# Hybrid attention and linear-attention step on one core: a ring of small weight slots, 512-wide products, and first sums over half of the mix

## The chip, the core and the metric

The kernel runs on one core of a Trainium2 chip. A core has five engines that work side by side, each through its own instructions in order: TensorE (PE, matrix products; PEld is its loading of the stationary operand), VectorE (DVE), ScalarE (ACT), GpSimd (POOL) and SyncE (SP), which issues most of the DMAs. They wait for each other through semaphores. The metric is the device time of one execution in microseconds (us). One further execution was recorded by the hardware profiler; times within the program are from that one.

## What is computed

Two layers over 2048 prompt tokens and 8 x 16 sample tokens, model width 1024. Each layer projects the normalised input into nine parts, runs sliding-window attention and gated linear attention side by side, multiplies both by gates, projects the joined result (the "mix") back, and adds a gated input embedding:

```python
xn = rms_norm(h, norm_g)
u = xn @ w_in
qa, ka, va, ga, qb, kb, vb, gb, ab = jnp.split(u, _split_points(), axis=-1)
...                                   # q and k: norm per head, partial rotary
oa = swa_prompt(qa, ka, va, sinks)    # or swa_sample with the cache
...
logg = jax.nn.log_sigmoid((ab @ w_gate_up + b_gate).astype(jnp.float32)) / GATE_TAU
ob, s_new = gla_recurrent(qb, kb, vb, logg, s0)
ob = rms_norm(ob, gla_norm_g)
mix = jnp.concatenate([oa.reshape(bn, L, A_WIDTH) * jax.nn.silu(ga),
                       ob.reshape(bn, L, B_WIDTH) * jax.nn.silu(gb)], axis=-1)
h = h + mix @ w_out
gate = jax.nn.sigmoid(rms_norm(h, pe_norm_g) @ w_pg)
h = h + gate * (p_l @ w_pe)
```

The widths of the parts are 512, 128, 128, 512, 256, 256, 512, 512 and 16 columns.

## The kernel before

**Tiling.** The 17 tiles of 128 tokens (the last one holds the samples) are worked off in five groups of 3, 4, 4, 3 and 3 tiles, for each of two layers; so there are ten groups and 34 passes of a tile. A group runs `phase_in` (projections, attention, linear attention) and then `phase_out` (output projection, gate).

**Products.** Every weight and every activation is split into a high and a low part, and every product runs as three matmuls per slice of 128 rows (k): high by high, high by low, low by high. These are the three source lines L343, L344 and L345 in `mm3`. With eight k a unit has 24 matmuls. `unit_b` holds 128 tokens stationary and streams weight columns (kv 272 wide; q0, q1, vb0, vb1, gb0, gb1 256 wide). `unit_a` holds 128 weight columns stationary and streams the group's 384 or 512 tokens (ga, qb, kb, and in `phase_out` o0 to o3 over the mix, g0 to g3 over the activations `A` and `B`, and e0 to e3 with two k over the embedding `phl`).

**Weights.** They come by DMA in pieces of two k by 256 columns (256 KB) into four `raw` buffers. `w_split` makes the high part on ScalarE (L175) and the low part on VectorE (L95). There are two whole-block buffers `w`, and two of the small ones `we`. `w_ahead` issues splits of the next block while the present one runs. From the end of the o blocks on, splits are held behind the last square of the mean (`wgate`).

**Order.** Attention and linear attention are generators that are advanced a step at a time (`pump`) between projection units. A list scheduler then sets each engine's instruction order from the program's order and its own estimates. Attention is finished (`drain`) after vb, linear attention after gb. A linear attention tile ends so: products into the PSUM pair `o` and state products into `t`; squares of `o` on ScalarE (L798, four); a scale and a power on GpSimd (L799, L801); four products into `on` on VectorE (L804); four transposes on TensorE (L815); then ScalarE (L817) and VectorE (L818) write them into the second half of the mix, `mix1`. The first half, `mix0`, is the attention's. PSUM has two banks for `mm`, two for `t`, and four that are used either as two pairs, `s` and `o`, or as four single banks `pw`.

Of the kernel before, what the change touches and what calls it, by code (L numbers as in the profile page):

```python
# [8 lines left out]
F32 = mybir.dt.float32  # L9
# [14 lines left out]
Z = dict(eg=0, gk=2, yp=1, ym=6, pga=1, pqk=1, pvb=2, pgb=3, pG=3, pgb0=0, lanes=2, keepk=1, keepq=-1, tga=2, wo=-1,  # L24
         y1=1, y2=1, y3=1, ya=1, yb=1, raw=4, hx=4, vbe=2, po0=6, wah=0, th=3)
# [21 lines left out]
def hybrid_step(ctx: ExitStack, tc: tile.TileContext, a: dict, o: dict):  # L47
# [54 lines left out]
    def pw(n=512):  # L102

        rot[0] += 1
        if rot[0] % 3 == 1:
            return pm(n)
        return banks["pool"].tile([128, 512], F32, tag="w", name="pw", bufs=4)[:, :n]
# [5 lines left out]
    def chain(prev, after=(), **kw):  # L113

        if prev[0] is None:
            prev[0] = PE.matmul(**kw).ins  # L116
# [10 lines left out]

    plan = []
    for l in range(DEPTH):
        for gi in range(len(GROUPS)):  # L130
            for nm, wd in IN_BLOCKS:
                off = IN_OFF[nm][0]
                plan.append((l, gi, nm, 8, wd, a["w_in"][l, :, off:off + 8 * wd].rearrange("p (k c) -> p k c", k=8)))
            for b in range(4):
                plan.append((l, gi, f"o{b}", 8, 256, a["w_out"][l, :, b]))
            for b in range(4):
                plan.append((l, gi, f"g{b}", 8, 256, a["w_pg"][l, :, b]))
                plan.append((l, gi, f"e{b}", 2, 256, a["w_pe"][l, :, b]))
    pieces = []
    for bi, (_, _, nm, K, wd, src) in enumerate(plan):  # L140
        for k0 in range(0, K, 2):
            pieces.append((bi, k0, src[:, k0:k0 + 2, :], wd))
# [5 lines left out]
    wtiles = {}  # L148
    raws = {}
    st = dict(dma=0, split=0, blk=0)  # L150
    wgate = [None]
    RAW = Z["raw"]

    def w_dma(upto):
        while st["dma"] < min(upto, len(pieces)):
            bi, k0, src, wd = pieces[st["dma"]]
# [5 lines left out]
    def w_split(n=1):  # L162
        for _ in range(n):
            i = st["split"]
            if i >= len(pieces):
                return
            bi, k0, _, wd = pieces[i]
            w_dma(i + RAW)
            if bi not in wtiles:
                K = plan[bi][3]  # L170
                wtiles[bi] = w_p.tile([128, 2, K, wd], F32R, tag="w" if K == 8 else "we", name="w", bufs=2)
            w = wtiles[bi]
            r = raws.pop(i)
            with tc.issue_after(wgate[0]) if wgate[0] is not None else ExitStack():
                A.activation(out=w[:, 0, k0:k0 + 2, :], in_=r, func=ACTF.Copy)  # L175
            ptt(w[:, 1, k0:k0 + 2, :], r, w[:, 0, k0:k0 + 2, :], ALU.subtract, V)
            st["split"] += 1
            w_dma(i + 1 + RAW)

    def w_get(l, gi, nm):  # L180
        bi = st["blk"]
        assert plan[bi][:3] == (l, gi, nm), (plan[bi][:3], l, gi, nm)
        while st["split"] <= last_piece[bi]:
            w_split()
        st["blk"] += 1
        return wtiles.pop(bi)

    def w_ahead(nblocks, frac):
# [6 lines left out]
        while st["split"] < min(tgt, last_piece[b1] + 1):  # L195
            w_split()
# [141 lines left out]
    def mm3(out, sides, gate=None):  # L338

        last = len(sides) - 1  # L340
        for i, (sh, sl, mh, ml) in enumerate(sides):
            with tc.issue_after(gate[1]) if gate is not None and i == gate[0] else ExitStack():
                PE.matmul(out=out, lhsT=sh, rhs=mh, start=(i == 0), stop=False)  # L343
            PE.matmul(out=out, lhsT=sh, rhs=ml, start=False, stop=False)  # L344
            lastmm[0] = PE.matmul(out=out, lhsT=sl, rhs=mh, start=False, stop=(i == last)).ins  # L345

    def unit_b(xt, w, ti, c0, cn, ps_=None):
        ps = (ps_ or pm)(cn)
        s = slice(ti * TT, ti * TT + TT)
        mm3(ps, [(xt[k // 4][:, k % 4, 0, s], xt[k // 4][:, k % 4, 1, s], w[:, 0, k, c0:c0 + cn], w[:, 1, k, c0:c0 + cn])  # L350
                 for k in range(KD)])
        return ps

    def unit_a(xt, w, m, s0, sn, ps_=None, gate=None):
        ps = (ps_ or pm)(sn)
        c = slice(m * 128, m * 128 + 128)
        mm3(ps, gate=gate, sides=[(w[:, 0, k, c], w[:, 1, k, c], xt[k // 4][:, k % 4, 0, s0:s0 + sn], xt[k // 4][:, k % 4, 1, s0:s0 + sn])
                 for k in range(KD)])
        return ps


    def phase_in(l, gi, ip, xn, mslot, S_in):
# [23 lines left out]
        def qk_norm(ps, nh, g, ti, y=None):  # L386
            t = tiles[ti]
            w = nh * 64
            sq = ip.tile([128, 256], F32, tag="qsq", name="qsq", bufs=1)
            A.activation(out=sq[:, :w], in_=ps[:, :w], func=ACTF.Square)  # L390
            rs = ip.tile([128, 4], F32, tag="qrs", name="qrs", bufs=2)
# [4 lines left out]
            if y is None:  # L396
                y = ip.tile([128, 4, 64], F32, tag="qy", name="qy", bufs=4)
# [3 lines left out]
            rt = ip.tile([128, 2, 4, 16], F32, tag="qrt", name="qrt", bufs=2)  # L401
# [15 lines left out]
        w = w_get(l, gi, "kv")  # L417
        if l == 0 and gi == 0:
            kvs = [pw(272) for _ in tiles]
            for k in range(KD):  # L420
                for ti in range(nt):
                    s = slice(ti * TT, ti * TT + TT)
                    xh, xl = xt[k // 4][:, k % 4, 0, s], xt[k // 4][:, k % 4, 1, s]
                    PE.matmul(out=kvs[ti], lhsT=xh, rhs=w[:, 0, k], start=(k == 0), stop=False)
                    PE.matmul(out=kvs[ti], lhsT=xh, rhs=w[:, 1, k], start=False, stop=False)
                    PE.matmul(out=kvs[ti], lhsT=xl, rhs=w[:, 0, k], start=False, stop=(k == KD - 1))
        for ti, t in enumerate(tiles):
            w_ahead(1, (ti + 1 + Z["wo"]) / nt)
            ps = kvs[ti] if l == 0 and gi == 0 else unit_b(xt, w, ti, 0, 272, pw)
            y = qk_norm(ps, 2, vec[:, l, V_GK:V_GK + 64], ti)  # L430
# [27 lines left out]
        for b in range(2):  # L458
            w = w_get(l, gi, f"q{b}")
            yq = ip.tile([128, 4, 4, 64], F32, tag="E", name="yq", bufs=2)  # L460
# [783 lines left out]
```

## Time and profile before

| | us |
|---|---|
| median of three runs | 2370.84 (2368.56 to 2370.91) |
| profiled execution, its own time | 2376.32 |
| its span in the trace | 2374.5 |
| TensorE busy | 2300.5 (97%) |
| VectorE busy | 1637.6 (69%) |
| ScalarE busy | 1302.4 (55%) |
| GpSimd busy | 683.5 (29%) |

The busy time of TensorE counts any time in which a matmul is under way. Matmuls overlap, so the time that one costs is read from the start of one to the start of the next, and idle time from the waits. Weights make up most of the DMA traffic, at a mean of 118 GB/s.

### The profile page before, as it was taken

How to read it: one execution, taken by the hardware profiler on the slowest of the kernel's cores; microseconds unless marked ns; L12 is line 12 of the kernel's file. 1: busy time of each engine (PE TensorE's matmuls, PEld its weight loads, DVE VectorE, ACT ScalarE, POOL GpSimd, SP SyncE). 2: the span in 40 equal slices, each digit the busy share in tenths (PEclk: the TensorE clock that was granted, in tenths of full speed). 3: DMA queues.
4: the chain of work that ended last, by engine and by line, in shares of the span. 5: the costliest groups of instructions: out<-in, count | busy, mean ns of one | idle time of the engine just before them, and what ended most of it. 6: DMA issues, size and time to landing. Idle time of an engine off the chain costs nothing.

```text
span 2374.5 us, 46429 instructions
## 1 busy us (share of the span) xinstructions
PE 2300.5 (97%) x17244; PEld 2094.9 (88%) x17244; DVE 1637.6 (69%) x3851; ACT 1302.4 (55%) x3083; POOL 683.5 (29%) x839
## 2 busy tenths in 40 slices
PE   7999999999999999999999999999999999999998
PEld 7999888898888989998999998887988889899988
DVE  7767765677567866775776687657766578577754
ACT  7546654545545655653665555545555456465543
POOL 4224212341214322422322161223312152133221
PEclk9999999999999999999999999999999999999999
DMA  4344323432154334534532542144321443354343
GB/s 147 108 132 152 98 72 99 134 117 90 37 161 144 106 95 158 153 107 141 165 114 72 167 149 84 54 137 130 99 72 64 146 148 107 102 157 139 107 141 100
DMA packets 160260, 279.29 MB, mean 118 GB/s; under 512 B 17649, under 2 KB 43633, under 8 KB 160033
## 3 DMA queue, kind: packets, MB, share of 16 engines
q1 hardware_dynamic: 159344, 275.43, 37.0%
q8 instruction: 136, 2.23, 0.4%
q10 hardware_dynamic: 688, 0.88, 0.1%
q14 instruction: 92, 0.75, 0.1%
HBM read 255.41 MB, written 20.71 MB: 116 GB/s over the span
## 4 chain that ended last, share of the span: by engine, by line
PE 79%; DVE 7%; ACT 6%; issue 3%; DMA 3%; POOL 2%; DVEq 0%; SPq 0%; POOLq 0%; ACTq 0%
PE mm L343 14%; PE mm L345 14%; PE mm L344 13%; PE pw L343 9%; PE pw L345 9%; PE pw L344 8%; PE o L122 3%; DVE w L95 3%; PE s L122 2%; PE s L116 1%; DMA raw<-in_w_out_dram 1%; PE o L116 1%; PE t L122 1%; ACT w L175 1%; PE t L556 1%
## 5 line engine op out<-in xcount | busy, mean ns | idle before, releaser
L95 DVE TENSOR_TENSOR w<-raw,w 128x512 fp32r<-128x512 f32 (+1 forms) x800 | 561.0, 743 | 61.9 <-ACT w L175 58.6
L175 ACT ACTIVATE w<-raw 128x512 fp32r<-128x512 f32 (+1 forms) x800 | 449.8, 624 | 204.3 <-PE mm L345 60.3
L343 PE MATMUL mm<-w,B 128*128 128x256 f32 (+1 forms) x688 | 200.2, 291 | 0.0
L344 PE MATMUL mm<-w,B 128*128 128x256 f32 (+1 forms) x688 | 196.3, 285 | 0.0
L345 PE MATMUL mm<-w,B 128*128 128x256 f32 (+1 forms) x688 | 196.1, 285 | 0.0
L343 PE MATMUL mm<-w,A 128*128 128x256 f32 (+1 forms) x664 | 193.3, 291 | 0.0
L344 PE MATMUL mm<-w,A 128*128 128x256 f32 (+1 forms) x664 | 189.8, 286 | 0.0
L345 PE MATMUL mm<-w,A 128*128 128x256 f32 (+1 forms) x664 | 189.4, 285 | 0.0
L95 POOL TENSOR_TENSOR ot<-gth,hst 128x384 f32<-128x384 f32 (+1 forms) x79 | 102.0, 1292 | 273.5 <-DVE gth L1050 203.0
L505 ACT ACTIVATE P<-s,nm 128x192 f32<-128x192 f32 (+3 forms) x272 | 108.9, 413 | 95.2 <-DVE nm L500 51.2
L343 PE MATMUL pw<-mix,w 128*128 128x384 f32 (+1 forms) x424 | 156.1, 370 | 0.0
L95 POOL TENSOR_TENSOR acc<-sq,acc 128x384 f32<-128x384 f32 (+1 forms) x60 | 75.8, 1264 | 277.9 <-ACT sq L274 274.8
L343 PE MATMUL mm<-B,w 128*128 128x384 f32 (+1 forms) x424 | 154.1, 363 | 1.1 <-DVE zm L975 1.0
L344 PE MATMUL pw<-mix,w 128*128 128x384 f32 (+1 forms) x424 | 155.1, 367 | 0.0
L345 PE MATMUL pw<-mix,w 128*128 128x384 f32 (+1 forms) x424 | 154.8, 367 | 0.0
L343 PE MATMUL mm<-A,w 128*128 128x384 f32 (+1 forms) x424 | 153.6, 362 | 0.0
L344 PE MATMUL mm<-A,w 128*128 128x384 f32 (+1 forms) x424 | 153.2, 361 | 0.0
L345 PE MATMUL mm<-A,w 128*128 128x384 f32 (+1 forms) x424 | 152.8, 360 | 0.0
L345 PE MATMUL mm<-B,w 128*128 128x384 f32 (+1 forms) x424 | 152.7, 360 | 0.0
L344 PE MATMUL mm<-B,w 128*128 128x384 f32 (+1 forms) x424 | 152.3, 359 | 0.0
L343 PEld LDWEIGHTS mm<-w,B 128*128 128x128 f32 x688 | 131.4, 191 | 5.9 <-issue 4.2
L345 PEld LDWEIGHTS mm<-w,B 128*128 128x128 f32 x688 | 131.3, 191 | 1.4 <-issue 1.3
(321 smaller groups left out, 6878.4 us busy)
## 6 DMA issues: line engine op xcount, KB each, us to landing
raw<-in_w_in_dram SPq DMA_DIRECT2D x400, 256.0 KB, 3.1
raw<-in_w_out_dram SPq DMA_DIRECT2D x160, 256.0 KB, 3.1
raw<-in_w_pg_dram SPq DMA_DIRECT2D x160, 256.0 KB, 3.8
raw<-in_w_in_dram SPq DMA_DIRECT2D x40, 272.0 KB, 3.1
raw<-in_w_pe_dram SPq DMA_DIRECT2D x40, 256.0 KB, 3.5
hl<-in_h_dram SPq DMA_DIRECT2D x24, 192.0 KB, 3.5
hbuf<-ot SPq DMA_DIRECT2D x24, 192.0 KB, 2.6
hx<-hbuf SPq DMA_DIRECT2D x24, 192.0 KB, 3.7
```

The lines of the kernel that those rows point to most:

```text
L95: (eng or G).tensor_tensor(out=out, in0=in0, in1=in1, op=op1)
L116: prev[0] = PE.matmul(**kw).ins
L122: prev[0] = PE.matmul(**kw).ins
L175: A.activation(out=w[:, 0, k0:k0 + 2, :], in_=r, func=ACTF.Copy)
L343: PE.matmul(out=out, lhsT=sh, rhs=mh, start=(i == 0), stop=False)
L344: PE.matmul(out=out, lhsT=sh, rhs=ml, start=False, stop=False)
L345: lastmm[0] = PE.matmul(out=out, lhsT=sl, rhs=mh, start=False, stop=(i == last)).ins
L505: A.activation(out=P[:, e, p0:p0 + wd], in_=ps[:, e // 2, e % 2, :wd], func=ACTF.Exp, scale=0.125, bias=nm[:, e:e + 1], accum_out=den[:, 0 ...
L556: PE.transpose(out=pf[:, 0, g, :], in_=Pc[:, 0:128], identity=ident)
```

## The change

It has four parts that hang together, and some small ones.

1. The weights of a block lie in slots of two k by 512 columns or four k by 256 columns, in a ring of five. A slot is given back as soon as the last unit of its block has used its last k (`end=True`, `freed`), and then the next pieces are split.
2. q, vb and gb are one block each of 512 columns; `unit_b` is 512 wide for them.
3. Linear attention steps stand in one queue with attention, without the `drain` after vb; the pairs `s` and `o` are guarded by a `lock`. The last tile's transposes are deferred (`done["tail"]`). The first four k (those of `mix0`) of the first four output tiles are computed as half sums `pss` around them, and `phase_out` adds the other four k.
4. In the last o block `w_ahead(2)` also covers the next block, so that e0 can be split ahead of the last squares.

Small ones: norm and rotary work on eight heads at once, q's transposes come four at a time, the gate chain is grouped by function and scans in place, the softmax negates its maximum in place, the first prompt tile's attention comes ahead of the sample's, `hl` has two buffers instead of three, and several tiles share a buffer tag.

```diff
-                plan.append((l, gi, nm, 8, wd, a["w_in"][l, :, off:off + 8 * wd].rearrange("p (k c) -> p k c", k=8)))
+            plan.append((l, gi, "kv", 8, [in_src(l, "kv")], 2, "w"))
+            plan.append((l, gi, "q", 8, [in_src(l, "q0"), in_src(l, "q1")], 2, "w"))
+            for nm in ("ga0", "ga1", "qb", "kb"):
+                plan.append((l, gi, nm, 8, [in_src(l, nm)], 4, "w"))
+            for nm in ("vb", "gb"):
+                plan.append((l, gi, nm, 8, [in_src(l, nm + "0"), in_src(l, nm + "1")], 2, "w"))
...
+    RING = dict(w=5, we=2)
...
+        def used(self, k):
+
+            if k % self.ks == self.ks - 1:
+                slots.pop((self.bi, k // self.ks))
+                held[self.tag] -= 1
...
+        if (bi, si) not in slots:
+            if held[tag] == RING[tag]:
+                return False
+            held[tag] += 1
+            slots[bi, si] = w_p.tile([128, 2, ks, sum(x.shape[2] for x in srcs)], F32R, tag=tag, name="w", bufs=RING[tag])
...
+    def freed(w, ahead, k0=0):
+
+        def f(i):
+            w.used(k0 + i)
+            for _ in range(ahead if (k0 + i) % 2 else 0):
+                w_split()
+        return f
...
+    def unit_b(xt, w, ti, cn, ps_=None, mid=None, end=False):
...
+        rel = freed(w, 2) if end else None
+
+        def after(i):
+            if rel is not None:
+                rel(i)
+            if mid is not None and i == 3:
+                mid()
...
+        if not is_sample(tiles[-1]):
+            jobs[-1:] = [later(lambda: gla_a(0)), jobs[-1], later(lambda: gla_a(1)), later(lambda: gla_b(0, sgbs)),
+                         later(lambda: gla_b(1, sgbs))] + [later(lambda ti=ti: gla(ti, sgbs)) for ti in order[2:]]
+        bg.extend(jobs)
...
+            while done["seq"] != ti or tag in lock:
+                if done["seq"] == ti and done["scores"] == nt and "s" not in lock:
+                    tag = "s"
+                    break
+                yield
+            lock.add(tag)
...
+            if ti == last_ti:
+                done["tail"] = lambda: gla_out(on, ti)
+                return
...
+            ps = unit_b(xt, w, ti, 512, mid=lambda: pump(Z["pvb"]), end=ti == nt - 1)
...
-        drain()
...
+        ws = [w_get(l, gi, f"o{b}") for b in range(2)]
+        pss = []
+        for mt in range(4):
+            if mt == 3:
+                with tc.issue_after(lastmm[0]):
+                    done["tail"]()
+            pss.append(unit_a(mixes, ws[mt // 2], mt % 2, 0, n, pm(n) if mt % 3 == 0 else pw1(n), ks=(0, 4), end=mt % 2 == 1))
...
+            w_ahead(2 if mt // 2 == 3 else 1, (m + 1 + Z["wah"]) / 2)
+            if mt < 4:
+                ps = unit_a(mixes, ws[mt // 2], m, 0, n, pss[mt], ks=(4, 8), end=m == 1)
+            else:
+                ps = unit_a(mixes, ws[mt // 2], m, 0, n, pw(n), end=m == 1)
```

**How it moves instructions.** A row gives line, operation, output and inputs with the program's own numbers, and in brackets the engines or DMA queues whose semaphores it waits for. In the kernel after, `mm3` is L382 to L384, the squares are L869, the transposes L886, their copies L888 and splits L212.

TensorE, first group, around the last linear attention tile. Before: its products into `o`, its state products, products of the first o unit, and then the transposes of `on`:

```order
L122 MATMUL o_1873<-S_1733,E_1736 128x128 x4
L122 MATMUL t_1882<-vb_1131,ke_1836 64x128 [waits PE_49]
L122 MATMUL t_1882<-vb_1131,ke_1836 64x128 x3
L345 MATMUL mm_1998<-mix0_220,w_1931 128x384
...
L815 MATMUL t_1903<-cst_72,on_1898 128x128 [waits DVE_49,PE_49]
L815 MATMUL t_1903<-cst_72,on_1898 128x128 [waits DVE_49] x3
```

After: the half sum of mt1 (`pw_1685`), then that of mt2 (`pw_1703`), then the transposes:

```order
L126 MATMUL o_1605<-S_1453,E_1478 128x128 x4
L126 MATMUL t_1614<-vb_1084,ke_1564 64x128 [waits PE_49]
L126 MATMUL t_1614<-vb_1084,ke_1564 64x128 x3
L382 MATMUL pw_1685<-mix0_223,w_1387 128x384
...
L382 MATMUL pw_1703<-mix0_223,w_1596 128x384 [waits DVE_49]
...
L886 MATMUL t_1716<-cst_72,on_1663 128x128 [waits PE_49]
L886 MATMUL t_1716<-cst_72,on_1663 128x128 x3
```

The wait for VectorE's `on` stood at the transposes and now stands at the first product of mt2's half sum, twelve matmuls ahead of them.

ScalarE at the same place. Before, four splits of o1 (`w_1950`) stand between the last silu and the tile's squares:

```order
L791 ACTIVATE ke_1836<-t_1833 128x256 [waits PE_49]
L817 ACTIVATE mix1_1683<-t_1838,vec_73 128x4x128 [waits PE_49]
L658 ACTIVATE th_1870<-mm_1845,cols_191 128x256 [waits DVE_49,PE_49]
L175 ACTIVATE w_1950<-raw_1934 128x512 [waits DMAHW2_49]
L175 ACTIVATE w_1950<-raw_1938 128x512 [waits DMAHW3_49]
L175 ACTIVATE w_1950<-raw_1942 128x512 [waits DMAHW4_49]
L175 ACTIVATE w_1950<-raw_1946 128x512 [waits DMAHW5_49]
L798 ACTIVATE gsq_1891,gss_1890<-o_1873 128x128 [waits PE_49,Activation_49,Pool_49]
L798 ACTIVATE gsq_1891,gss_1890<-o_1873 128x128 [waits Activation_49] x3
L817 ACTIVATE mix1_1683<-t_1903,vec_73 128x4x128 [waits PE_49]
```

After:

```order
L862 ACTIVATE ke_1564<-t_1561 128x256 [waits PE_49]
L888 ACTIVATE mix1_1470<-t_1566,vec_73 128x4x128 [waits PE_49]
L869 ACTIVATE gsq_1656,gss_1655<-o_1605 128x128 [waits PE_49,DVE_49,Activation_49,Pool_49]
L869 ACTIVATE gsq_1656,gss_1655<-o_1605 128x128 [waits Activation_49] x3
L212 ACTIVATE w_1698<-raw_1631 128x512 [waits DMAHW0_49,PE_49]
L212 ACTIVATE w_1698<-raw_1635 128x512 [waits DMAHW1_49]
L212 ACTIVATE w_1740<-raw_1646 128x512 [waits DMAHW2_49,DVE_49,PE_49]
L212 ACTIVATE w_1740<-raw_1650 128x512 [waits DMAHW3_49]
L888 ACTIVATE mix1_1470<-t_1716,vec_73 128x4x128 [waits PE_49]
```

The squares moved ahead of the four splits; straight ahead of them is now the copy of the tile before.

ScalarE at the end of the first group's o blocks. Before, with e0's split `w_2284`:

```order
L1024 ACTIVATE A1_1930<-hst_1918,vec_73 128x384 [waits DVE_49]
L274 ACTIVATE sq_2278<-hst_1918 128x384 [waits Pool_49]
L175 ACTIVATE w_2284<-raw_2198 128x512 [waits DMAHW7_49]
L175 ACTIVATE w_2289<-raw_2202 128x512 [waits DMAHW0_49,PE_49]
L175 ACTIVATE w_2289<-raw_2244 128x512 [waits DMAHW1_49]
```

After, with e0's split `w_1931`:

```order
L313 ACTIVATE sq_1888<-hst_1749 128x384 [waits Pool_49]
L212 ACTIVATE w_1931<-raw_1850 128x512 [waits DMAHW5_49]
L212 ACTIVATE w_1910<-raw_1801 128x512 [waits DMAHW1_49,PE_49]
L212 ACTIVATE w_1910<-raw_1839 128x512 [waits DMAHW2_49]
L212 ACTIVATE w_1987<-raw_1902 128x512 [waits DMAHW6_49,PE_49]
L1132 ACTIVATE A1_1761<-hst_1749,vec_73 128x384 [waits DVE_49]
L313 ACTIVATE sq_1939<-hst_1749 128x384 [waits Pool_49]
```

e0's split moved from behind the last square to a place three squares ahead of it.

## Rows read from the trace of the kernel before

**Rows 1.** The page, busy time of each engine and its share.

```profile
PE 2300.5 (97%) x17244; PEld 2094.9 (88%) x17244; DVE 1637.6 (69%) x3851; ACT 1302.4 (55%) x3083; POOL 683.5 (29%) x839
PE 79%; DVE 7%; ACT 6%; issue 3%; DMA 3%; POOL 2%; DVEq 0%; SPq 0%; POOLq 0%; ACTq 0%
```

**Rows 2.** Groups of L343 by form: names, shapes, count | busy us, mean ns.

```profile
L343 PE MATMUL mm<-w,B 128*128 128x256 f32 x648 | 188.6, 291 | 0.0
L343 PE MATMUL mm<-w,A 128*128 128x256 f32 x624 | 181.7, 291 | 0.0
L343 PE MATMUL pw<-w,A 128*128 128x256 f32 x192 | 55.7, 290 | 0.0
L343 PE MATMUL pw<-w,B 128*128 128x256 f32 x168 | 48.0, 286 | 0.0
```

**Rows 3.** TensorE's timeline (start, duration, line, names, shape): first and last of three runs.

```profile
177.03 0.33 PE L343 MATMUL mm<-mix,w 128*128 128x384 f32 x1
...
180.49 0.34 PE L345 MATMUL mm<-mix,w 128*128 128x384 f32 x1
...
262.08 0.29 PE L344 MATMUL mm<-w,B 128*128 128x256 f32 x1
...
264.71 0.28 PE L345 MATMUL mm<-w,B 128*128 128x256 f32 x1
...
410.02 0.39 PE L344 MATMUL mm<-mix,w 128*128 128x512 f32 x1
...
415.91 0.39 PE L343 MATMUL pw<-mix,w 128*128 128x512 f32 x1
```

**Rows 4.** Waits of TensorE: who ended them: us in total, times, longest.

```profile
PE t L815 <- DVE on L804: 26.3, 9, 3.9
PE pw L343 <- ACT w L175: 9.5, 5, 2.6
PE pw L345 <- DVE w L95: 3.9, 4, 1.3
```

**Rows 5.** Timelines at the last linear attention tile, first and second group.

```profile
140.55 0.72 PE L122 MATMUL o<-S,E 64*128 64x128 f32 x8
...
142.22 1.28 ACT L175 ACTIVATE w<-raw 128x512 fp32r<-128x512 f32 x2 [1.30 <-DMA raw<-in_w_out_dram]
...
144.77 0.19 ACT L798 ACTIVATION_READ_ACCUMULATOR gsq<-o 128x1 f32 x1
...
145.50 1.01 POOL L801 TENSOR_TENSOR gss<-gss,mhalf 128x4 f32<-128x4 f32 x1
...
146.54 1.13 DVE L804 SCALAR_TENSOR_TENSOR on<-o,gss,sgb 128x128 f32<-128x128 f32 x4 [1.84 <-POOL gss L801]
...
147.04 1.01 PE L815 MATMUL t<-cst,on 128*128 128x128 f32 x4 [3.23 <-DVE on L804]
...
391.62 0.50 PE L122 MATMUL o<-S,E 64*128 64x128 f32 x6
...
398.02 1.01 PE L815 MATMUL t<-cst,on 128*128 128x128 f32 x4 [2.36 <-DVE on L804]
```

**Rows 6.** Windows (us, PE, PEld, DVE, ACT, POOL busy, PEclk, DMA): the first of nine.

```profile
148.20:151.60 3.40, 3.40 (x13) 3.40 (x12) 1.71 (x2) 1.42 (x2) 0.00 (x0) 0.50 0.99 326
```

**Rows 7.** Timelines of ScalarE and TensorE behind the first group's o blocks.

```profile
182.40 2.18 ACT L175 ACTIVATE w<-raw 128x512 fp32r<-128x512 f32 x4
...
183.06 0.45 PE L343 MATMUL pw<-phl,w 128*128 128x384 f32 x1 [2.23 <-ACT w L175]
```

**Rows 8.** A split on ScalarE and VectorE, a piece's DMA (KB, us), the q window.

```profile
L175 ACT ACTIVATE w<-raw 128x512 fp32r<-128x512 f32 x760 | 426.0, 623 | 199.0 <-PE mm L345 60.3 <-PE pw L345 47.7 <-DMA raw<-in_w_pe_dram 37.8
L95 DVE TENSOR_TENSOR w<-raw,w 128x512 fp32r<-128x512 f32 x760 | 527.7, 736 | 61.9 <-ACT w L175 58.6
raw<-in_w_in_dram SPq DMA_DIRECT2D x400, 256.0 KB, 3.1
239.60:265.20 25.60, 25.60 (x217) 25.51 (x215) 22.09 (x88) 14.77 (x40) 13.66 (x22) 1.00 0.27 83
```

More of the change, by code (lines that the diff above doesn't have):

```diff
@@ L111, in pair, with chain @@
         return banks["pool"].tile([128, 2, 512], F32, tag=tag, name=tag, bufs=1)
-    def chain(prev, after=(), **kw):
+    def chain(prev, after=(), behind=None, **kw):
         if prev[0] is None:
-            prev[0] = PE.matmul(**kw).ins
+            with tc.issue_after(behind) if behind is not None else ExitStack():
+                prev[0] = PE.matmul(**kw).ins
             for x in after:
@@ L147, in hybrid_step @@
         last_piece[p[0]] = i
-    wtiles = {}
+    slots = {}
     raws = {}
+    held = dict(w=0, we=0)
     st = dict(dma=0, split=0, blk=0)
@@ L160, in w_dma, with w_split @@
             st["dma"] += 1
[L162 to L178, printed above, removed]
+    def w_split():
+        i = st["split"]
+        if i >= len(pieces):
+            return False
+        bi, si, kk, c0, wd, _ = pieces[i]
+        _, _, _, _, srcs, ks, tag = plan[bi]
+        if (bi, si) not in slots:
+            if held[tag] == RING[tag]:
+                return False
+            held[tag] += 1
+            slots[bi, si] = w_p.tile([128, 2, ks, sum(x.shape[2] for x in srcs)], F32R, tag=tag, name="w", bufs=RING[tag])
+        w_dma(i + RAW)
+        w = slots[bi, si]
+        r = raws.pop(i)
+        hi, lo = (w[:, x, kk:kk + 2, c0:c0 + wd] for x in range(2))
+        with tc.issue_after(wgate[0]) if wgate[0] is not None else ExitStack():
+            A.activation(out=hi, in_=r, func=ACTF.Copy)
+        ptt(lo, r, hi, ALU.subtract, V)
+        st["split"] += 1
+        w_dma(i + 1 + RAW)
+        return True
     def w_get(l, gi, nm):
@@ L336, in hybrid_step, with mm3 @@
     prog = [0]
-    def mm3(out, sides, gate=None):
-        last = len(sides) - 1
+    def mm3(out, sides, gate=None, first=True, last=True, after=None):
+        n = len(sides) - 1
         for i, (sh, sl, mh, ml) in enumerate(sides):
             with tc.issue_after(gate[1]) if gate is not None and i == gate[0] else ExitStack():
-                PE.matmul(out=out, lhsT=sh, rhs=mh, start=(i == 0), stop=False)
+                PE.matmul(out=out, lhsT=sh, rhs=mh, start=first and i == 0, stop=False)
@@ L344, in mm3 @@
             PE.matmul(out=out, lhsT=sh, rhs=ml, start=False, stop=False)
-            lastmm[0] = PE.matmul(out=out, lhsT=sl, rhs=mh, start=False, stop=(i == last)).ins
-    def unit_b(xt, w, ti, c0, cn, ps_=None):
+            lastmm[0] = PE.matmul(out=out, lhsT=sl, rhs=mh, start=False, stop=last and i == n).ins
+            if after is not None:
+                after(i)
+    def freed(w, ahead, k0=0):
[4 more added lines that the diff above has]
+        return f
@@ L356, in unit_a @@
+    def unit_a(xt, w, m, s0, sn, ps=None, gate=None, ks=(0, KD), end=False):
         c = slice(m * 128, m * 128 + 128)
-        mm3(ps, gate=gate, sides=[(w[:, 0, k, c], w[:, 1, k, c], xt[k // 4][:, k % 4, 0, s0:s0 + sn], xt[k // 4][:, k % 4, 1, s0:s0 + sn])
-                 for k in range(KD)])
+        mm3(ps, gate=gate, first=ks[0] == 0, last=ks[1] == KD, after=freed(w, 1, ks[0]) if end else None,
+            sides=[(w(0, k, c), w(1, k, c), xt[k // 4][:, k % 4, 0, s0:s0 + sn], xt[k // 4][:, k % 4, 1, s0:s0 + sn])
+                   for k in range(*ks)])
```

314 lines of the change are left out of this document (174 added, 140 removed).

## The prediction, made before the changed kernel was run

> **What bounds the kernel now.** I read the page's busy times and chain first, then the groups of TensorE by form, its waits, and last the rows around the two longest kinds of wait. TensorE is busy 97% of the span, the next engine, VectorE, 69%, and the chain that ended last is TensorE for 79% [rows 1]. So the time is the sum of TensorE's products plus the few tens of microseconds in which it stands still; work taken off other engines counts only where TensorE waits for it. I therefore price three things: how long one product takes from its start to the next one's start, the waits that the change touches, and new waits for weights that arrive in smaller slots.
>
> **A: products 512 wide.** The products whose tokens are stationary run 256 columns wide in q0, q1, vb0, vb1, gb0 and gb1. By form they are 648 + 624 + 192 + 168 for the first of the three source lines, as many for each of the other two, so 4896 [rows 2]; that is 6 blocks x 34 token tiles x 24. The change halves their number, to 2448 of 512 columns. The cost of one is the step from start to start, since durations overlap. 23 starts of 256-wide products in a row run from 262.08 to 264.71, 22 steps of 0.1195 us; 27 of 512-wide ones from 410.02 to 415.91, 26 steps of 0.2265; 21 of 384-wide ones from 177.03 to 180.49, 20 steps of 0.173 [rows 3]. Doubling the columns thus costs 0.107 us more, not 0.1195: some 13 ns of each step do not grow with the columns, and 384 lies on the same line (0.1195 + 0.0535 = 0.173). Before: 4896 x 0.1195 = 585.1 us; after: 2448 x 0.2265 = 554.5 us. **A = -30.6 us**, all of it on TensorE. The trace has 512-wide steps only with weights stationary; token-stationary ones are seen 256 wide alone, so the bounds are 0 (a step that doubles with the columns) and -33 (if a 512-wide step lost a further ns). I take -30.6, the row itself.
> The Trainium skill, page "TensorE: Matmul & The Clock Gate", section "Back-to-back issue gap", states a step of N/2.4 + 2.5 ns for the isolated product. By that the saving would be an estimated 2448 x 2.5 ns = 6.1 us; the rows show about 13 ns where it has 2.5, so the measurement decides here, and the page's figure is kept as a rival below.
>
> **B: the last linear attention tile of a group.** Before phase_out's first product with the mix's second half, TensorE waits for `on` in nine of ten groups, 26.3 us in total and 3.9 at most [rows 4]. In the first group the tile's last product into `o` ends at 140.55 + 0.72 = 141.27. ScalarE's squares of it should follow at once, but two splits of o1's weights, which wait for their DMA, stand ahead of them and end at 143.50. The squares end at 144.96, GpSimd at 146.51, `on` at 147.67, and the transposes start at 147.04 after 3.23 us of standing still [rows 5]. The order of the program shows that the change does not move more products into this gap: behind the last `o` stand the state products and one half sum of twelve (before: ten to twelve products), and then the half sum of mt2, whose bank is one that the last `o` lay in and which therefore waits for the last `on`. What does change is ScalarE's row: the squares stand ahead of those splits. Without the delay squares end at about 142.9, GpSimd 1.55 later at 144.4, `on` 1.16 later at 145.6; TensorE is through its 12 x 0.173 = 2.1 us by 143.9, so it waits 1.7 instead of 3.23, a gain of 1.5. In the second group the last `o` ends at 392.12 and the wait ends at 398.02 [rows 5]; the undisturbed sum 392.12 + 1.6 + 1.55 + 1.16 = 396.4 makes that 1.5 earlier too. Nine such gains are 13 us; but a copy of the tile before now stands straight ahead of the squares, and groups that waited less can gain less. **B = -7 us**, half of it. Bounds: -34, if all 26.3 go and with them the low clock behind them: nine stretches of 3.4 us in the body run at half the granted clock, seven of them behind such waits, and 13 products take 3.40 there instead of 13 x 0.173 = 2.25, 1.15 more [rows 6]; and +6, if the delay stays and all ten groups wait for the last `on` instead of the first, 0.6 later.
>
> **C: from the output to the gate products.** ScalarE splits the first block of the input embedding, e0, behind the last square, and TensorE waits: in the first group the split stands at 182.40 and e0's product starts at 183.06 after 2.23 us idle [rows 7]. Five such waits sum to 9.5 us [rows 4]. With w_ahead(2) in the last output block e0's split comes ahead of the last squares, and TensorE goes on with e0 and then with the gate product. Next late is the last copy of A, which that product needs at its last step; between the two lie 31 products of 0.173, 5.4 us, against an addition, a copy and a difference of about 2 us, so it stays hidden. One of the low-clock stretches lies behind such a wait, 1.15. **C = -11 us**; bounds 0 (the split is early, but a wait for A takes its place) and -15 (the 3.9 us for the second half of splits go too [rows 4]).
>
> **D: new waits for weights.** A 512-wide block fills four of five slots, and a slot is given back only in the block's last unit. A slot of two k lasts 6 x 0.2265 = 1.36 us, so slots come free 1.36, 2.72 and 4.08 us into that unit, and the next unit wants them at 6.8, 8.2 and 9.5. Refilling one takes two splits on ScalarE of 0.623 and two on VectorE of 0.736, about 2.0 us, and, once the four landed pieces are used, a DMA of 3.1 [rows 8]. By hand: second slot ready at 3.4, third at 4.8; the fourth's pieces land at 5.8 and 6.5, ready at 7.9, against 9.5. Smallest margin 1.6 us. It holds if the splits are not held up on their own engines, and VectorE is busy 22.09 of 25.60 us in the q stage [rows 8]. **D = +3 us**: three late splits out of 50 such boundaries (five in each of ten groups) at about 1 us, the size of today's split waits, 3.9 / 4 [rows 4]. Bounds: -4, if those of today go, and +26 (20 boundaries around q at the 1.3 us of the longest [rows 4]).
>
> **Nothing** I count for the rest: norm and rotary steps on wide tiles, four transposes at once, the gate chain by function, one small softmax step less, the missing drain, the locks on banks. They are on engines that are 55 to 69% busy [rows 1] beside TensorE's products; if that cover fails, a wait costs like those of rows 4, 1 to 2 us each, and I allow 3 either way. DMA volume is the same.
>
> **Sum**, against the profiled execution's own 2376.3 us: -30.6 - 7 - 11 + 3 = -45.6, so 2330.7. That execution is 5.5 us over the median of the runs; taken from the median, 2370.8 - 45.6 = **2325**.
>
> **Rivals.**
> 1. *The last tile's wait goes altogether.* The other 19.3 us of B and 8 us of low clock come too: 2325 - 27 = 2298. For it: the half sums exist to fill this gap, and a scheduler may start them in another order on the chip's times. Against it: the bank that mt2 shares with the last `o`, in all ten groups.
> 2. *Slower: the ring starves TensorE.* Every boundary has to refill three slots in one burst, on engines that run their instructions in order. If a burst starts 3.1 us (a landing [rows 8]) beyond plan, less the margin of 1.6, each of 50 boundaries costs 1.5: 2325 + 75 = 2400. It decides from a mean of (2370.8 - 2325 + 3) / 50 = 1.0 us per boundary. For it: VectorE's load in the q stage; against it: margins of 3.4 us for two of three slots, and splits that already ran at this rate on average.
> 3. *The ring costs something, but only around q:* D at its bound of 26 instead of 3, so 2348. The point is a VectorE that lags more than 1.6 us at 20 of the boundaries.
> 4. *A wide product costs twice a narrow one*, so that the step is set by columns, and only a few ns each are saved. With 6 us of A left the time is 2325 + 24.5 = 2350; with none, 2356. The 384 and 512 rows speak against it, the lack of a wide token-stationary row for it.
>
> **How the numbers follow.** Forecast (A whole, B and C in part, D small) 0.63, own range 2315 to 2340: B from 0 to -13, C from -15 to -5, D from 0 to +10. Rival 1: 0.13. Rival 3: 0.10. Rival 4: 0.07. Rival 2: 0.05. A mixture of rivals 2 and 3 that just eats the gain: 0.02. A range from 2298 to 2353 holds the forecast, rivals 3 and 4, and half of rival 1: 0.63 + 0.10 + 0.07 + 0.06 = 0.86, less 0.05 for sizes outside. A measurement of this kernel tells about 0.2% (4.7 us) from no change. Faster by more than that: the forecast and rivals 1, 3 and 4, 0.93; within it 0.02; slower, rival 2, 0.05.
>
> **What would show it.** A: 512-wide token-stationary products start 0.2265 us apart, 2448 of them. B: the wait of TensorE for `on` moves from the transposes to the first product of mt2's half sum, about ten waits of 1 to 2.5 us; squares start right behind the last `o`. C: no idle time ahead of e0's first product. D: waits of TensorE for ScalarE's or VectorE's `w` in front of q, ga0, vb, gb and o0 stay under 10 us in all. I am wrong if the wide step is over 0.235, if waits for `w` exceed 25 us, or if waits for `on` are still 26 or are gone.

## The result, and the profile after

The changed kernel takes 2342.34 us (median of four runs, 2341.43 to 2345.76), the kernel before on the same chip 2370.88. The ratio is 0.9883, with a 95% interval of 0.9866 to 0.9900: 28.5 us faster, where 45.8 were forecast. The profiled execution took 2341.45 us; against the profiled one of before that is 34.9 us, since that one lay 5.5 us over its median and this one 0.9 under.

The page after, busy times and chain, to be set beside [rows 1]; line numbers are now those of the changed file (`mm3` L382 to L384, `on` L875, transposes of `on` L886, splits L212, S L924):

```profile
PE 2261.6 (97%) x14796; PEld 1946.8 (83%) x14796; DVE 1622.7 (69%) x3579; ACT 1271.1 (54%) x2927; POOL 679.8 (29%) x771
...
PE 77%; DVE 6%; issue 6%; DMA 4%; ACT 4%; POOL 3%; DVEq 0%; ACTq 0%; POOLq 0%; SPq 0%
```

TensorE has 2448 matmuls fewer and still decides the end. Its waits, to be set beside [rows 4] (total, times, longest):

```profile
PE pw L382 <- DVE on L875: 12.0, 10, 1.9
PE t L886 <- DVE on L875: 7.8, 4, 2.7
PE mm L480 <- ACT w L212: 7.8, 1, 7.8
PE t L860 <- DVE S L924: 6.6, 4, 1.7
PE t L498 <- DVE abT L501: 5.4, 2, 3.8
PE s L120 <- issue: 4.6, 2, 2.9
PE t L860 <- DVE mix L889: 4.5, 4, 1.3
...
PE pw L383 <- DVE w L95: 0.4, 2, 0.2
```

The wait for `on` stands at mt2's half sum in all ten groups, as read from the order; there it is 12.0 us. The other 7.8 stand in the two groups with samples, in front of the transposes of the tiles ahead of the last. Together that is 19.8 us instead of 26.3: in the eight groups without samples the wait fell from 18.9 to 9.0, in the two with samples it rose from 7.4 to 10.8. The squares of the last tile now start 0.2 us behind its last product into `o` (0.5 in two groups); before it was up to 3.6. The waits for weights are gone except at the program's start (the 7.8, which was there before too). New are the waits in front of L860, the transposes of the next tile's `ke`, for VectorE to read a bank `t` (S and mix, 11.1 us in the eight groups without samples); those in front of L120 and L498 also grew.

The wide products, as groups and as a run in the timeline, beside [rows 2] and [rows 3]:

```profile
L382 PE MATMUL mm<-w,A 128*128 128x512 f32 x328 | 130.3, 397 | 0.0
L382 PE MATMUL mm<-w,B 128*128 128x512 f32 x328 | 130.2, 397 | 0.0
L382 PE MATMUL pw<-w,A 128*128 128x512 f32 x80 | 31.5, 398 | 0.0
L382 PE MATMUL pw<-w,B 128*128 128x512 f32 x80 | 31.2, 394 | 0.0
...
339.65 0.39 PE L384 MATMUL mm<-w,B 128*128 128x512 f32 x1
...
341.69 0.39 PE L384 MATMUL mm<-w,B 128*128 128x512 f32 x1
```

816 per line, 2448 in all; ten starts from 339.65 to 341.69 are nine steps of 0.2267 us. Term A's price is met.

So the products became some 30 us shorter, the waits for weights 14 us, the wait for `on` 6.5, and yet TensorE's waits sum to 72.8 us after against 68.8 before. To see where that arises I measured each group's length in the trace, from its first kv product to the next group's. In us, profiled executions; the columns to the right are experiments told of below:

| groups | before | changed | e4 (same program) | e1 | e5 | e6 | e9 | e12 |
|---|---|---|---|---|---|---|---|---|
| four of 4 tiles | 1074.7 | 1046.5 | 1046.9 | 1065.2 | 1051.7 | 1066.7 | 1040.8 | 1056.6 |
| three of 3 tiles | 628.6 | 616.8 | 619.4 | 605.8 | 617.9 | 608.0 | 614.6 | 605.3 |
| two with samples | 439.2 | 442.5 | 440.2 | 433.3 | 434.4 | 440.8 | 434.2 | 432.5 |
| the first | 219.7 | 221.3 | 221.6 | 218.8 | 221.9 | 223.4 | 222.7 | 218.2 |
| sum | 2362.2 | 2327.1 | 2328.0 | 2323.1 | 2325.9 | 2338.9 | 2312.3 | 2312.6 |

The columns "changed" and e4 are the same program; a row differs by up to 2.6 us between them. The gain lies in the groups of four tiles (28) and of three (12). The sample groups and the first are no shorter, though their wide products save 0.9 us per tile there as everywhere.

### The profile page after: what moved, and what is told of

It is laid out like the page before. It is cut to its first block, busy times and chain, and to the rows that moved or that the text cites. A ratio compares the mean times of both kernels' runs of the same rounds, so it can differ in the third digit from the quotient of the medians.

```text
span 2339.7 us, 41130 instructions
## 1 busy us (share of the span) xinstructions
PE 2261.6 (97%) x14796; PEld 1946.8 (83%) x14796; DVE 1622.7 (69%) x3579; ACT 1271.1 (54%) x2927; POOL 679.8 (29%) x771
## 4 chain that ended last, share of the span: by engine, by line
PE 77%; DVE 6%; issue 6%; DMA 4%; ACT 4%; POOL 3%; DVEq 0%; ACTq 0%; POOLq 0%; SPq 0%
PE mm L382 15%; PE mm L384 14%; PE mm L383 14%; PE pw L382 7%; PE pw L383 7%; PE pw L384 7%; PE o L126 3%; DVE w L95 2%; DMA raw<-in_w_pe_dram 2%; PE s L120 2%; PE s L126 2%; POOL xacc L95 1%; DMA raw<-in_w_out_dram 1%; ACT w L212 1%; PE o L120 1%
## 5 line engine op out<-in xcount | busy, mean ns | idle before, releaser
L95 DVE TENSOR_TENSOR w<-raw,w 128x512 fp32r<-128x512 f32 (+1 forms) x800 | 575.3, 744 | 141.1 <-ACT w L212 136.3
L212 ACT ACTIVATE w<-raw 128x512 fp32r<-128x512 f32 (+1 forms) x800 | 471.4, 626 | 240.8 <-PE pw L384 62.5
L382 PE MATMUL mm<-B,w 128*128 128x384 f32 (+1 forms) x432 | 156.3, 362 | 1.8 <-DVE gth L1154 1.1
L382 PE MATMUL mm<-A,w 128*128 128x384 f32 (+1 forms) x432 | 155.6, 360 | 1.9 <-DVE gth L1154 1.3
L384 PE MATMUL mm<-B,w 128*128 128x384 f32 (+1 forms) x432 | 156.1, 361 | 0.0
L383 PE MATMUL mm<-B,w 128*128 128x384 f32 (+1 forms) x432 | 155.9, 361 | 0.0
L384 PE MATMUL mm<-A,w 128*128 128x384 f32 (+1 forms) x432 | 155.6, 360 | 0.0
L383 PE MATMUL mm<-A,w 128*128 128x384 f32 (+1 forms) x432 | 155.0, 359 | 0.0
L382 PE MATMUL pw<-mix,w 128*128 128x384 f32 (+1 forms) x384 | 138.4, 366 | 12.0 <-DVE on L875 12.0
L382 PE MATMUL mm<-w,B 128*128 128x512 f32 (+1 forms) x368 | 141.7, 385 | 0.0
L383 PE MATMUL mm<-w,B 128*128 128x512 f32 (+1 forms) x368 | 141.3, 384 | 0.0
L384 PE MATMUL mm<-w,B 128*128 128x512 f32 (+1 forms) x368 | 140.8, 383 | 0.0
L382 PE MATMUL mm<-w,A 128*128 128x512 f32 (+1 forms) x360 | 139.5, 387 | 0.0
L383 PE MATMUL mm<-w,A 128*128 128x512 f32 (+1 forms) x360 | 138.8, 385 | 0.0
L384 PE MATMUL mm<-w,A 128*128 128x512 f32 (+1 forms) x360 | 138.3, 384 | 0.0
L384 PE MATMUL pw<-mix,w 128*128 128x384 f32 (+1 forms) x384 | 137.4, 358 | 0.0
L383 PE MATMUL pw<-mix,w 128*128 128x384 f32 (+1 forms) x384 | 137.3, 357 | 0.0
L95 POOL TENSOR_TENSOR mix<-ga_t,mix 128x512 fp32r<-128x512 f32 x34 | 53.0, 1560 | 265.6 <-ACT mix L583 265.6
L563 ACT ACTIVATE P<-s,mx 128x192 f32<-128x192 f32 (+3 forms) x272 | 108.7, 412 | 8.6 <-DVE mx L559 8.4
L1155 ACT ACTIVATE gth<-gth 128x384 f32<-128x384 f32 (+2 forms) x81 | 45.0, 560 | 125.7 <-DVE gth L1154 125.5
```

The costliest lines, as they stand in the source:

```text
L95: (eng or G).tensor_tensor(out=out, in0=in0, in1=in1, op=op1)
L212: A.activation(out=hi, in_=r, func=ACTF.Copy)
L382: PE.matmul(out=out, lhsT=sh, rhs=mh, start=first and i == 0, stop=False)
L563: A.activation(out=P[:, e, p0:p0 + wd], in_=ps[:, e // 2, e % 2, :wd], func=ACTF.Exp, scale=0.125, bias=mx[:, e:e + 1], accum_out=den[:, 0 ...
L1155: ta = A.activation(out=th[:, c], in_=th[:, c], func=ACTF.Tanh, scale=0.5)
```

## The experiments

All are edits of the changed kernel, except for what is said. Ratios are to the kernel before on the same chip, whose median was 2375 to 2377 there; the intervals are 0.001 to 0.002 wide on either side. e1 to e8 and e12 ran on one chip, e9 to e11 on another. All experiments change the scheduler's order as well as the thing named; that is a limit of each of them.

**e4, w_ahead(1) in the last o block.**

```diff
-            w_ahead(2 if mt // 2 == 3 else 1, (m + 1 + Z["wah"]) / 2)
+            w_ahead(1, (m + 1 + Z["wah"]) / 2)
```

> Undoes term C alone: in the last o block w_ahead covers one block, so that e0 is split behind the last square. If the early split is what took the waits for w away (9.5 us, and some of the 3.9), 2351 to 2356. If TensorE then waits no more than now, 2342.

Measured: 2342.18 us, ratio 0.9860. The program that comes out is the changed one, instruction for instruction on every engine. So the step that put e0's early split down to `w_ahead(2)` names the wrong line: the splits that `freed` issues as slots come free have already gone past e0. The run is worth more as a yardstick. One program gave a ratio of 0.9883 for the result and 0.9860 here. Its own time is the same (2342.34 and 2342.18 us); it is the kernel before that took 2370.88 there and 2376.58 here, so that the change is worth 34.4 us here. Differences of 5.5 us between ratios from different sets of runs therefore say nothing, and the experiments are compared with e4.

**e7, e0's split held behind the last square.** The splits stop at e0's first piece until the last square of the o blocks is issued.

```diff
+        limit[0] = first_piece[[p[:3] for p in plan].index((l, gi, "e0"))]
         for mt in range(KD):
...
         wgate[0] = sqi
+        limit[0] = 10 ** 9
```

> The split of e0 and all splits behind it are held until the last square of the o blocks is issued; e4 showed that w_ahead(2) alone does not move it. If the early split is what took away 9.5 us of waits for w and some of the 3.9, those come back at 2.2 to 2.7 us in each group of three or more: 10 to 20 us, ratio 0.992 to 0.996. If TensorE then waits for the squares' sum or for A instead, under 5 us.

Measured: 2362.53 us, ratio 0.9948, 20 us slower than e4. The wait of [rows 7] is back (timeline of TensorE in the fourth group, and the kernel's waits):

```profile
920.25 0.69 PE L383 MATMUL pw<-phl,w 128*128 128x384 f32 x1 [2.23 <-ACT w L213]
...
PE mm L383 <- DVE gth L1157: 9.8, 3, 4.9
PE pw L383 <- DVE gth L1157: 8.6, 6, 2.8
...
PE pw L383 <- ACT w L213: 4.5, 2, 2.2
```

The waits for `w` are only 4.5 us of it; the rest stands in front of later gate products, for `gth` (18.4 against 5.7 in the changed kernel at the same line, and 8.9 there at all lines). The edit holds back all splits behind e0 too, so it prices all early splits together: about 20 us.

**e8, the tail not deferred.** The last tile's transposes come ahead of the half sums.

```diff
+        done["tail"]()
         ws = [w_get(l, gi, f"o{b}") for b in range(2)]
         pss = []
         for mt in range(4):
-            if mt == 3:
-                with tc.issue_after(lastmm[0]):
-                    done["tail"]()
```

> The last tile's transposes come ahead of the half sums instead of behind the third. If the half sums are what covers the wait for on, the cover of 12 to 24 products (2 to 5 us) is gone in ten groups: 15 to 30 us more, ratio 0.995 to 1.001. If the scheduler moves the half sums ahead anyway, 0.988.

Measured: 2373.42 us, ratio 0.9993 (0.9982 to 1.0003): with this one edit nothing is left of the whole change. The wait, and one of its places in the fourth group:

```profile
PE t L886 <- DVE on L875: 36.1, 14, 3.5
...
894.92 1.16 PE L886 MATMUL t<-cst,on 128*128 128x128 f32 x4 [3.23 <-DVE on L875]
```

36.1 us against 19.8, and 89.4 us of waits in all against 72.8. TensorE's busy time is 13.4 us longer as well (2275.0 against 2261.6), at a mean granted clock of 0.989 against 0.995. The deferred tail with half sums around it is worth about 31 us against e4, four times what term B gave it.

**e1, all three wide blocks issued in halves.** Slots, units and half sums stay; each wide product becomes two of 256 columns.

```diff
+        for k in range(KD):
+            for h in range(2):
+                c = slice(256 * h, 256 * h + 256)
+                PE.matmul(out=ps[:, c], lhsT=xh, rhs=w(0, k, c), start=(k == 0 and h == 0), stop=False)
...
+            after(k)
```

> The changed kernel with every 512-wide token-stationary product issued as two of 256 columns into the same bank; slots, order of units, half sums and splits stay. If the width alone gave term A, the 2448 extra products cost 2 x 0.1195 - 0.2265 us each, 30.6 us: 2373. If the width gave less than half of that, because other engines set the pace of those stages, under 2357.

Measured: 2336.47 us, ratio 0.9834 (0.9819 to 0.9848). The first expectation fails. The bound of the second, under 2357, is met, but neither foresaw a gain: 2448 more products, and the kernel is not slower but some 6 us faster than e4. TensorE's busy time is 19.0 us longer than in the changed kernel (2280.6 against 2261.6), its waits are 23.4 us less (49.4 in all). The table shows where: in groups of four tiles the halves cost 18.7 us, as the products say and more; in those of three tiles they gain 11.0, with samples 9.2, in the first 2.5.

One group of three tiles (the fourth of the layer) shows how. Windows from its qk products to the o blocks and from there to the gate (us, busy of PE, PEld, DVE, ACT, POOL, PEclk, DMA, GB/s), first in the changed kernel, then in e1:

```profile
799.60:869.00 69.40, 68.43 (x521) 56.05 (x521) 47.41 (x129) 37.60 (x104) 15.92 (x20) 1.00 0.26 80
869.00:913.80 44.80, 41.37 (x319) 39.33 (x318) 30.26 (x52) 22.51 (x53) 11.27 (x13) 1.00 0.55 179
```

```profile
804.90:879.20 74.30, 74.30 (x760) 67.66 (x759) 51.20 (x138) 41.31 (x117) 18.24 (x24) 1.00 0.28 86
879.20:915.80 36.60, 36.60 (x227) 35.97 (x226) 25.12 (x46) 19.56 (x42) 7.26 (x7) 1.00 0.60 190
```

The changed kernel is at the o blocks 4.9 us sooner and pays 8.2 behind it: 114.2 us in all against 110.9. In the two windows of the changed kernel TensorE stands still for 4.4 us, in e1 not at all, and that is more than the difference. The work of the last tiles has not become shorter with the products; it now falls into the o blocks, where 319 matmuls lie instead of 227. The last tile's products into `o`, set beside the group's first output product, show it too (changed kernel, then the kernel before):

```profile
869.03 0.33 PE L382 MATMUL mm<-mix,w 128*128 128x384 f32 x1
...
880.99 0.72 PE L126 MATMUL o<-S,E 64*128 64x128 f32 x8
```

```profile
881.73 0.34 PE L343 MATMUL mm<-mix,w 128*128 128x384 f32 x1
...
883.07 0.71 PE L122 MATMUL o<-S,E 64*128 64x128 f32 x8
```

They end 12.7 us behind it, before 2.0. Over the ten groups it is 12 to 21 us in the changed kernel, 2 at most before, and 7 at most in e1, so most of the shift goes with the width. What holds the work up there is seen on ScalarE and VectorE, in the changed kernel:

```profile
872.76 0.66 PE L126 MATMUL t<-vb,ke 128*64 128x128 f32 x8
872.35 0.63 ACT L212 ACTIVATE w<-raw 128x512 fp32r<-128x512 f32 x1 [1.91 <-DMA raw<-in_w_out_dram]
873.25 0.63 ACT L212 ACTIVATE w<-raw 128x512 fp32r<-128x512 f32 x1 [0.27 <-DMA raw<-in_w_out_dram]
874.55 0.63 ACT L212 ACTIVATE w<-raw 128x512 fp32r<-128x512 f32 x1 [0.67 <-DMA raw<-in_w_out_dram]
875.09 0.26 ACT L869 ACTIVATE gsq<-o 128x128 f32<-128x128 f32 x1
...
875.21 0.69 DVE L95 TENSOR_TENSOR w<-raw,w 128x512 fp32r<-128x512 f32 x1 [0.61 <-ACT w L212]
875.82 0.60 DVE L924 SCALAR_TENSOR_TENSOR S<-S,dec,t 128x128 f32<-128x128 f32 x2
...
876.57 0.41 PE L860 MATMUL t<-cst,E 128*128 128x128 f32 x2 [1.70 <-DVE S L924]
```

and in e1 (its S is L934, its squares L879):

```profile
875.50 0.66 PE L126 MATMUL t<-vb,ke 128*64 128x128 f32 x8
...
875.68 0.28 ACT L879 ACTIVATE gsq<-o 128x128 f32<-128x128 f32 x1 [1.65 <-PE o L126]
...
876.21 0.61 DVE L934 SCALAR_TENSOR_TENSOR S<-S,dec,t 128x128 f32<-128x128 f32 x2 [0.88 <-PE t L126]
...
877.53 0.44 PE L870 MATMUL t<-cst,E 128*128 128x128 f32 x2
```

In the changed kernel the state products end at 873.42, but S starts at 875.82, behind splits that wait for their DMA, and the squares likewise. In e1 the same splits were done in time; squares and S follow at once, and L870 waits for nothing. It is the delay of [rows 5] again, moved from the last tile to the one before. But it does not stand in the groups of three tiles alone. In the second group, one of four tiles:

```profile
384.21 0.63 ACT L212 ACTIVATE w<-raw 128x512 fp32r<-128x512 f32 x1 [0.77 <-DMA raw<-in_w_out_dram]
...
386.00 0.66 PE L126 MATMUL t<-vb,ke 128*64 128x128 f32 x8
...
388.10 0.27 ACT L869 ACTIVATE gsq<-o 128x128 f32<-128x128 f32 x1
...
388.55 0.44 PE L860 MATMUL t<-cst,E 128*128 128x128 f32 x2 [1.04 <-DVE mix L889]
...
389.01 0.60 DVE L924 SCALAR_TENSOR_TENSOR S<-S,dec,t 128x128 f32<-128x128 f32 x2
```

S starts 2.35 us behind its products here and 2.40 in the fourth group; over the eight groups without samples it is 2.3 to 2.6. Yet TensorE loses only 1.0 us at L860 here and 0.6 at mt2, and in e1 the groups of four have a wait of their own, 2.1 to 2.2 us each for `sgb`, the silu of gb:

```profile
PE mm L382 <- DVE sgb L739: 10.2, 6, 2.2
```

So the groups differ in what TensorE loses by the delay, not in the delay. The splits on VectorE do not tell the two kernels apart either: idle time ahead of a split, 61.9 us before [rows 8], is now

```profile
L95 DVE TENSOR_TENSOR w<-raw,w 128x512 fp32r<-128x512 f32 (+1 forms) x800 | 575.3, 744 | 141.1 <-ACT w L212 136.3
```

and 155.3 in e1, which is faster.

**e5 and e6, halves in q alone, and in vb and gb alone.**

```diff
+        if cn < 512 or plan[w.bi][2] not in ('q',):      # e6: ('vb', 'gb')
+            mm3(ps, ...)
```

> The changed kernel with q alone issued in products of 256 columns (816 of 512 become 1632), vb and gb as changed. In q no chain of small products follows that sets the end, so the width should count in full: 816 x 12.5 ns = 10.2 us more than the changed kernel, ratio to before 0.9926. If the width gains nothing anywhere, the ratio of the changed kernel, 0.988.

> q 512 wide, vb and gb issued 256 wide. Theory chain: from vb to the first output products the linear attention chain and not TensorE sets the end, and with finer products the scheduler fits it in earlier, as in e1; then this is faster than e1 by q's 10.2 us: ratio to before 0.979. Theory luck of e1's q stage: the gain of e1 came from the order in q; then the ratio is above that of the changed kernel, 0.996 (20.4 us more products).

Measured: e5 2337.85 us, ratio 0.9845; e6 2348.92 us, ratio 0.9891. Neither theory's number was met: e5 did not lose its 10.2 us but is level with e4 or slightly faster, and e6 is 7 us slower, far from 0.979. By the table, the sample groups gain from q's halves (440.2 to 434.4), the groups of three tiles from those of vb and gb (619.4 to 608.0), and the groups of four lose by both: 4.8 us by q's, which is what the products cost (16 tiles x 24 x 12.5 ns), and 19.8 by those of vb and gb, twice what they cost. The two do not add up to e1 (sum 2325.9 and 2338.9 against 2323.1, from 2328.0).

**e3, the gate chain one q tile later.**

```diff
-            if ti == 0:
+            if ti == 1:
                 late.append(lambda: gate_chain(l, ip, nt, n, subs, abT, bs, tiles))
```

> The gate chain is queued behind the second q tile's product instead of the first's, so its two products (L1073) come a unit later. If their waits for abT (1.65 us in three groups and the first group's) are a loss, 3 to 6 us go: 2336 to 2339. If the q stage is paced by VectorE, nothing changes or the chain's late end costs up to 5 us more.

Measured: 2335.50 us, ratio 0.9828 (0.9812 to 0.9844), 7 us faster than e4. So one of the things that I counted at nothing cost that much where it stood: the kernel before queued the chain behind the last tile of q0, half way through q, the changed one queues it behind the first tile. The waits for `abT` in front of its products, at which the edit was aimed, fall from 4.3 to 1.8 us; the gain lies in the groups with samples (430.9 us against 440.0 in e4), while those of three tiles are longer (624.0 against 619.4).

**e2, an own place for the transposes of ke.**

```diff
-            pk = pt([128, 256])
+            pk = ss[:, 0, 256:]          # ss = pair("s")
```

> The transposes of ke (L860) go into the unused half of the pair s instead of a bank t. In the changed kernel TensorE waits 1.2 to 1.9 us ahead of them in each of ten groups, 15.6 us by start-to-start times, for VectorE's S or mix to have read the bank t. If that wait is a loss of its own, 10 to 15 us go: 2328 to 2332. If it only stands in for the wait on the last tile's chain, the waits for on grow by as much and the time stays within 3 us of 2342.

Measured: 2351.02 us, ratio 0.9889, 7 to 9 us slower than e4 (one of its four runs, 2343.17, is level with it). Both expectations fail. The wait for S at this place is gone, and others stand instead:

```profile
PE o L120 <- DVE ga_t L582: 5.4, 8, 1.0
...
PE o L120 <- DVE on L876: 5.2, 4, 1.3
...
PE s L861 <- DVE at L858: 4.7, 4, 1.4
PE t L126 <- POOL km L962: 4.6, 7, 1.3
```

So taking the bank's wait away was no gain: waits for VectorE and GpSimd came in its place.

**e9 and e12, a shorter chain from o to on.** The power on GpSimd left out, in the changed kernel (e9) and in e1 (e12).

```diff
-            G.tensor_scalar(out=ss, in0=ss, scalar1=cols[:, 3, ti:ti + 1], scalar2=cols[:, 4, ti:ti + 1],
-                            op0=ALU.mult, op1=ALU.add)
-            G.tensor_tensor(out=ss, in0=ss, in1=mhalf[:, 0:4], op=ALU.pow)
+            G.tensor_scalar(out=ss, in0=ss, scalar1=0.0, scalar2=0.001, op0=ALU.mult, op1=ALU.add)
```

> The changed kernel without the power on GpSimd (1.0 us) in the linear attention's norm; its scale is a constant, so the mix and all that follows from it is left wrong. It shortens the chain from o to on by about 1.1 us per tile. Theory chain: TensorE's ten waits for on in front of mt2's half sum (12.0 us) fall by about 1 us each, and those in the sample groups too: 10 to 15 us less, ratio 0.982 to 0.984. Theory order: what stands still is set by where the scheduler put the instructions, not by the chain's length; then within 4 us of the changed kernel, ratio 0.986 to 0.990.

> e1 (all three blocks issued 256 wide) and e9 (no power on GpSimd, a constant scale, so the mix and all behind it is left wrong) together. Theory chain: the linear attention chain is what eats the width's gain; shortened by 1.1 us per tile it lets go of the wide kernel more than of the narrow one, which waits for it less (3.7 us for on against 19.8). Then this gains under 10 us on e1, ratio 0.979 to 0.983, not better than e9. Theory order: the narrow products fit in better whatever the chain's length, and this is as far below e9 as e1 is below the changed kernel (0.5%): 0.974 or less.

Measured: e9 2325.45 us, ratio 0.9788; e12 2326.69 us, ratio 0.9787. The waits in e9:

```profile
PE t L860 <- DVE S L922: 9.3, 4, 2.8
...
PE t L884 <- DVE on L873: 4.3, 4, 2.8
...
PE pw L382 <- DVE on L873: 2.6, 6, 0.7
```

The ten waits for `on` fell from 12.0 to 2.6, about 1 us each as the chain theory said, and the time by 17 us against e4 (on another chip, but by the ratios too), more than its 10 to 15: GpSimd is busy 29% of the span, and an instruction of about 1 us on it, 34 times, is worth half its busy time. In e1 the same cut gains 10 to 11 us, at the edge of the 10 expected, and the halves are no longer ahead: 2312.6 against 2312.3 in the table. But there the chain theory ends. Even with the short chain the groups of three tiles are 9.3 us longer with wide products (614.6 against 605.3; 11.0 with the long chain), and those of four are 15.8 shorter. The loss in the small groups is for the most part not the norm's chain.

**e10 and e11, combinations.** e1 with e3, and e3 with vb and gb in halves.

> Both single edits that were faster than the changed kernel: all three blocks issued 256 wide (e1) and the gate chain one q tile later (e3). If their gains are of different stages they add: ratio 0.9834 - 0.0055 = 0.978. If both take away the same wait in the q stage, no better than e1 or e3: 0.983.

> q 512 wide with the gate chain one tile later (e3), vb and gb issued 256 wide (e6). q's width then costs no wait any more and its 10.2 us come in: better than e10 by up to 10 us, ratio down to 0.974. If the chip's time follows the order that the scheduler happens to find, anywhere from 0.975 to 0.990, and above e10.

Measured: e10 2338.53 us, ratio 0.9842, no better than e1 or e3; e11 2351.32 us, ratio 0.9901, at the upper edge of its second expectation. The gains don't add. Of the kernels that compute the whole result e1 and e3 are the best that I found, both faster than the kernel before and, on the same chip, by 6 to 7 us than the changed one; the two can't be told apart, and e5 lies within 2.4 us of them.

## Why the prediction was right and wrong

The sign and the range held; the forecast's own range, 2315 to 2340, was missed by 2 us. The size was 62% of the forecast (28.5 of 45.8 us), or 75% by e4's runs (34.4). Point by point:

**A** was right in its price and wrong in its worth. The steps are 0.2267 us, so the products are shorter by what was said. The step that failed is "all of it on TensorE": undoing the width did not lengthen the kernel but shortened it by 6 us (e1), so the net worth of A's 30.6 us is nothing, or a loss of 6 us. It pays in groups of four tiles (e1 against changed: 18.7 us, where the products alone give 16 x 0.9 = 14.4) and is more than lost in the others. I priced the products and did not ask whether the attention and linear attention work that runs beside them would still be covered when they are shorter.

**B** was right in where the wait stands and why it got shorter: the squares follow the last `o` at once, and the first group's wait at mt2 is 1.6 us where 1.7 was worked out. That the total came out so close, -6.5 against -7, is in part luck: it is made of -9.9 in the eight groups without samples and +3.4 in the two with them, which B did not treat apart. And the wait's worth was misread. "The change does not move more products into this gap" compared positions in the kernel before with positions in the kernel after. In the kernel after, the last tiles end later relative to the products (in the fourth group 13 us into the o blocks), so without the half sums the wait would not be 26.3 but 36.1 (e8). The deferred tail with its half sums earns about 31 us; that much of this only repairs what the shorter products did is read from these positions, and no run took the half sums out of e1.

**C** was right in sign and place, and low: about 20 us (e7, which holds back more splits than C spoke of) against 11, past its bound of 15. The cause is the ring's own splits, not `w_ahead(2)` (e4), and half of what e7 lost stands in waits for `gth` further on, which C did not count.

**D** was right for TensorE: waits for `w` under 1 us apart from the start. Rivals 2 and 3 did not happen. What I left out is what is queued behind a split on its own engines. I named DMA and splits as a chain that ends at TensorE; the squares and S stand behind them, and TensorE waits for those.

**The rest**, counted at nothing with 3 us either way, is the term that was mis-sized. The waits at L860 (11.1 us, none before), at the group's start and in the sample groups belong to it; e3 shows 7 us for the gate chain's place alone.

Rival 1 and rival 4 did not happen either: `on` is still waited for, and a wide product costs less than two narrow ones.

The worths do not add up: by e8 and e7 the deferred tail and the early splits earn 31 and 20 us, by e1 the width loses 6, and the whole change is worth 34.4 beside the same runs. Each is a worth with all the others in place.

What stays open is why exactly the groups of three tiles lose by the width. The timelines above show splits that wait for DMA ahead of squares and S in the wide form and not in the narrow one, but the same delay stands in the groups of four, which gain. It was read, not tested: no run took those splits away at that place. The scheduler's order changes with every edit, and its share can't be separated from these runs.

## What to carry to other kernels

Ask of a saving on the busiest engine what it was covering: if a chain on other engines runs beside it with a length of its own, the saving can come back as waits behind it. A wait has a worth only in its own program: price a filler such as the half sums against the program without it, not against the kernel before. And where transfers feed an engine that runs in order, look at what is queued behind the instruction that waits for the transfer, not only at who uses its result.

## What the runs showed of the hardware

A 512-wide product with tokens stationary starts 0.2267 us behind the one before it, as those with weights stationary did (0.2265 [rows 3]). The mean granted clock of TensorE is 0.995 after against 0.991 before, 0.997 in e12 and 0.989 in e8. That is the order of TensorE's total waits (72.8, 68.8, 40.3 and 89.4 us) except for the first two; after the change the waits for `on` are more, but shorter (2.7 us at most, 3.9 before [rows 4]). A power on 128x4 elements takes GpSimd 1.01 us [rows 5]; leaving it out 34 times took 17 us off the time (e9). One program with the same time gave ratios 0.0023 apart beside two sets of runs of the kernel before, more than the half width of either interval.
